# Two-layer hybrid encoder block on Trainium2: values and state products of the delta rule scan formed ahead of its steps, attention scores by pairs of heads on halves of the array

## The chip, the cores and the metric

The kernel runs on one core of one Trainium2 chip. The metric is the device time in microseconds of one execution; the median of three timed runs is given, and beside it one profiled execution.

## What is computed

Two layers over 512 tokens of width 1024. Each has a mixer of three head groups (a gated MLP, a dilated windowed attention with 6 heads, a bidirectional gated delta rule with 6 heads), an output projection, an expert layer (16 experts of 64 tokens) and a gated embedding. The change touches the delta rule and the attention. The delta rule, for one direction and per chunk of tokens (the reference uses chunks of 64, the kernel of 32):

```python
t_inv = lax.linalg.triangular_solve(lower + eye, jnp.broadcast_to(eye, lower.shape),
                                    left_side=True, lower=True, unit_diagonal=True)
u = t_inv @ (vc * bc[..., None])
w = t_inv @ (k_beta * jnp.exp(gc)[..., None])
qk = jnp.where(incl, jnp.einsum('bhntd,bhnsd->bhnts', qc, kc) * decay, 0.0)

def step(state, inp):
    q_n, k_n, u_n, w_n, g_n, qk_n = inp
    v_new = u_n - w_n @ state
    o_n = (q_n * jnp.exp(g_n)[..., None]) @ state + qk_n @ v_new
    g_last = g_n[..., -1:]
    state = state * jnp.exp(g_last)[..., None] + jnp.einsum(
        'bhtd,bhte->bhde', k_n * jnp.exp(g_last - g_n)[..., None], v_new)
    return state, o_n
```

It runs over the sequence forward and, with its own gates, backward; the two outputs are added, normalized by head and gated. The attention normalizes and rotates q and k, and its three patterns amount to one softmax over 512 keys with a fixed additive mask (`amask`), times v.

## The kernel before, in words

Tokens lie in four tiles (`t`) of 128 partitions. A projection is done in three matmuls per weight block (`mm3`): weights and activations are split in a high and a low part (`whi`, `wlo`, `xh`, `xl`), ScalarE forming the high part and GpSimd subtracting for the low one (L338, L340). Weights stream from HBM on SP's queue, each load issued when a buffer is free. Twelve buffers of 8 KB per partition ("slot") hold activations and weights in turn, two more ("gslot") the scan's operands.

The mixer of a layer goes: norm, the gated MLP, the decay terms (`gate_decay`), the delta rule's q, k, v with their short convolution (`gdn_qkv`), the products within chunks (`gdn_chunk`: pD is the decay's exponent, pG the products of k with k and of k with q), the inverse of the triangular matrices by a loop of 30 rounds on VectorE (`gdn_inv`), attention's q and k (`attn_qk`), and the transpose of the inverse (`gdn_inv_T`, tile XT).

Then two things run interleaved by `interleave`. The leading one is `gdn_scan`, 16 steps, each handling one chunk of the forward and one of the backward direction for all heads. A step: pK (L937) is k and q times the state St; tm (L940) scales it by the decay EG; rr (L944) is the values less k's part; pV (L951) multiplies by the inverse XT; vn (L955, ScalarE) copies it out; pS (L966) multiplies by the decayed k (kdec) and is added to the state, which GpSimd has decayed meanwhile (L961, L970); pO (L977) is the product within the chunk, added to q's part of tm for the output (L985, L987, L988). The filling one is a chain of attn_v (the value projection), core (the attention: scores sc L625, mask and maximum L629, exponential, scaling L634, four transposes ptp L640, and po L649 for two heads) and w_out_first (the first five blocks of the output projection, op). A fill piece returns a nominal cost, a scan piece the amount of fill owed after it (FILLS), and pieces are taken until at most 0.5 is owed; three fill pieces go first. The order so found is the order on TensorE: no piece starts ahead of the last matmul of the piece before it. After the scan come what is left of the fill, the group norm `gdn_out` (squares, `rsqrt`, two products, three transposes a tile) and `w_out_last`. The expert layer then has its own loads, which need the buffers of the mixer.

Of q, the head pair's two halves lie in two copies with the other head's 64 rows zero (L482, L483, L509, L510), so that each head's scores use all 128 rows against the shared k tile.

## Time and profile before

| | |
|---|---|
| median of 3 timed runs | 1956.84 us (1956.04 to 1957.46) |
| profiled execution | 1962.08 us, span 1960.3 us |
| mean granted TensorE clock | 0.95 |
| busy: TensorE, VectorE, ScalarE, GpSimd | 1809.5, 931.7, 523.9, 457.4 us |
| chain that ended last | TensorE 69%, VectorE 20%, ScalarE 3%, issue 3%, GpSimd 2%, DMA 2% |
| read from HBM | 461 MB |

Layer 0 takes 0 to 985 us of the span and layer 1 the rest. In layer 0 the scan and its fill run from 228 to about 400, the router to 449, where the experts' first product starts (449.7); these and the gated embedding last to 985. Busy is the time in which an engine has an instruction in work; matmuls are pipelined, so the start of one instruction to the start of the next is the price of one. A float32 matmul shows as two instructions, so 24 instructions are 12 products.

### The profile page before, as it was taken

The numbers are of one execution on the slowest core, as the hardware profiler recorded it, in microseconds if no ns is written. First come the engines' busy times: TensorE is split into PE (matmuls) and PEld (weight loads), VectorE is DVE, ScalarE is ACT, GpSimd is POOL, SyncE is SP. The second block draws the span as 40 slices with busy tenths as digits, with TensorE's granted clock in tenths as the row PEclk, the third lists the DMA queues.
The fourth block names the chain that finished last, engine by engine and source line by source line (L and its number), as shares of the span: only waits on it lengthen the run. The fifth ranks groups of instructions, "written<-read, shape, count | busy, mean of one in ns | idle before, by whom it ended". The sixth has DMA issues, their size and how long they took to land.

```text
span 1960.3 us, 30038 instructions
## 1 busy us (share of the span) xinstructions
PE 1809.5 (92%) x12216; PEld 1140.4 (58%) x12216; DVE 931.7 (48%) x2088; ACT 523.9 (27%) x1213; POOL 457.4 (23%) x402
## 2 busy tenths in 40 slices
PE   6898698979999999999989978899799999999999
PEld 5777665864344444434988767568544344443358
DVE  5879767671112121132778796776511212114126
ACT  4334444331010101102443344552311011011023
POOL 3544313320000003021645452233100000031025
PEclk9998788989999999999998977999799999999999
DMA  5212020187799999899342020202987999998991
GB/s 169 86 33 60 17 85 15 56 329 302 321 423 421 409 421 407 345 412 379 111 134 76 24 74 2 97 2 102 411 321 318 422 421 397 422 394 345 380 328 66
DMA packets 122394, 467.47 MB, mean 238 GB/s; under 512 B 11664, under 2 KB 68496, under 8 KB 75920
## 3 DMA queue, kind: packets, MB, share of 16 engines
q1 hardware_dynamic: 115168, 458.46, 59.5%
q10 hardware_dynamic: 7088, 7.09, 1.2%
q8 instruction: 96, 1.57, 0.3%
q14 instruction: 42, 0.34, 0.1%
HBM read 461.32 MB, written 4.19 MB: 237 GB/s over the span
## 4 chain that ended last, share of the span: by engine, by line
PE 69%; DVE 20%; ACT 3%; issue 3%; POOL 2%; DMA 2%; ACTq 0%; SPq 0%; DVEq 0%; POOLq 0%
PE pGt L1276 14%; PE pUp L1276 11%; PE pY L1276 10%; DVE acc L778 3%; PE xep L1206 2%; PE ysc L1295 2%; DVE rr L944 2%; PE xep L1207 2%; PE pY L1391 2%; PE pV L951 1%; PE op L348 1%; PE ysc L1296 1%; PE pgp L348 1%; PE pgp L350 1%; PE plep L1172 1%
## 5 line engine op out<-in xcount | busy, mean ns | idle before, releaser
L1276 PE MATMUL pGt<-w,xe 128*64 128x512 f32 x592 | 194.8, 607 | 0.0
L340 POOL TENSOR_TENSOR wlo<-w,whi 128x512 fp32r<-128x512 f32 (+5 forms) x66 | 162.1, 2473 | 102.9 <-ACT whi L338 71.9
L1276 PE MATMUL pUp<-w,xe 128*64 128x512 f32 x688 | 178.4, 593 | 0.0
L1343 POOL TENSOR_TENSOR x<-x,hh 128x1024 f32<-128x1024 f32 x8 | 18.8, 2356 | 620.0 <-DMA wx<-in_w_e_up_dram 310.4
L1276 PE MATMUL pY<-w,hidT 128*64 128x512 f32 x608 | 162.5, 596 | 0.2 <-ACT hidT L1350 0.2
L1360 DVE SCALAR_TENSOR_TENSOR yl<-pY,gsl,yh 128x512 fp32r<-128x512 f32 x28 | 21.0, 751 | 203.1 <-ACT yh L1359 201.5
L1301 DVE TENSOR_TENSOR x<-ysc,x 128x512 f32<-128x512 f32 x96 | 62.9, 686 | 110.5 <-PE ysc L1296 110.5
L1276 PEld LDWEIGHTS pUp<-w,xe 128*64 128x64 f32 x688 | 62.9, 137 | 89.5 <-issue 86.3
L1276 PEld LDWEIGHTS pGt<-w,xe 128*64 128x64 f32 x592 | 56.1, 137 | 99.2 <-issue 92.7
L1276 PE MATMUL pGt<-wx,xe 128*64 128x512 f32 x384 | 113.0, 599 | 0.3
L1334 DVE SCALAR_TENSOR_TENSOR hid<-sg,gsl,pUp 128x512 f32<-128x512 f32 x32 | 23.9, 748 | 169.8 <-PE pUp L1276 168.0
L1276 PEld LDWEIGHTS pY<-w,hidT 128*64 128x64 f32 x608 | 55.6, 136 | 76.2 <-issue 73.3
L1276 PE MATMUL pUp<-wx,xe 128*64 128x512 f32 x320 | 99.8, 595 | 0.0
L1276 PE MATMUL pY<-wx,hidT 128*64 128x512 f32 x288 | 86.2, 595 | 0.0
L1327 DVE SCALAR_TENSOR_TENSOR sg<-sg,pGt 128x512 f32<-128x512 f32 x32 | 21.7, 686 | 131.3 <-ACT sg L1326 131.3
L338 ACT ACTIVATE whi<-w 128x512 fp32r<-128x512 f32 (+5 forms) x66 | 68.2, 1058 | 38.5 <-PE op L349 15.8
L1326 ACT ACTIVATE sg<-pGt,gsl 128x512 f32<-128x512 f32 x32 | 21.8, 687 | 196.5 <-PE pGt L1276 194.6
L1350 ACT ACTIVATE hidT<-htp 128x512 f32<-128x512 f32 x32 | 19.0, 597 | 200.4 <-PE htp L1349 200.4
L1206 PE MATMUL xep<-OH,hh 128*128 128x256 f32 x256 | 70.1, 307 | 2.4 <-DVE OH L1194 2.4
L778 DVE SCALAR_TENSOR_TENSOR acc<-raw,pp,acc 128x512 f32<-128x512 f32 x72 | 64.3, 894 | 15.5 <-ACT acc L776 13.0
L348 PE MATMUL pgp<-whi,gTh 128*128 128x256 f32 x256 | 70.9, 281 | 0.0
L350 PE MATMUL pgp<-whi,gTl 128*128 128x256 f32 x256 | 69.8, 282 | 0.3 <-DVE gTl L279 0.3
(404 smaller groups left out, 4277.3 us busy)
## 6 DMA issues: line engine op xcount, KB each, us to landing
w<-in_w_e_up_dram SPq DMA_DIRECT2D x86, 1024.0 KB, 15.4
w<-in_w_e_down_dram SPq DMA_DIRECT2D x76, 1024.0 KB, 12.7
w<-in_w_e_gate_dram SPq DMA_DIRECT2D x74, 1024.0 KB, 15.6
wx<-in_w_e_gate_dram SPq DMA_DIRECT2D x48, 1024.0 KB, 9.9
wx<-in_w_e_up_dram SPq DMA_DIRECT2D x40, 1024.0 KB, 16.7
wx<-in_w_e_down_dram SPq DMA_DIRECT2D x36, 1024.0 KB, 12.0
wd<-in_w_e_down_dram SPq DMA_DIRECT2D x32, 512.0 KB, 8.3
w<-in_w_in_dram SPq DMA_DIRECT2D x14, 1024.0 KB, 5.2
```

Of the source, the lines that this page charges most:

```text
L338: self.nc.scalar.activation(rr_(hi[:, ks, :]), wk, AF.Copy)
L340: e.tensor_tensor(rr_(lo[:, ks, :]), wk, hi[:, ks, :], op=ALU.subtract)
L348: pe.matmul(p, lh, rh, start=first, stop=False)
L350: pe.matmul(p, ll, rh, start=False, stop=last)
L778: v.scalar_tensor_tensor(acc, raw[:, kk:kk + S], conv[:, b, kk:kk + 1], acc, op0=ALU.mult, op1=ALU.add)
L944: v.tensor_tensor(rr[kl[dr], :], vtok[kl[dr], tl, :], fl(tm[kl[dr]]), op=ALU.subtract)
L1206: pe.matmul(p, rr_(hh[:, t, ks]), OHf[:, t, :], start=(t == 0), stop=False)
L1207: pe.matmul(p, rr_(hl[:, t, ks]), OHf[:, t, :], start=False, stop=(t == NT - 1))
L1276: pe.matmul(pt[nh][64 * ei:64 * ei + 64, :], lhs[:, kk, 64 * ei:64 * ei + 64], wt[ei][k][:, nh * 512:nh * 512 + 512], start=(kk == 0), sto ...
L1295: pe.matmul(p, rr_(OT[:, t, :]), rr_(yh[:, ns]), start=True, stop=False)
L1301: v.tensor_tensor(xv, p, xv, op=ALU.add)
L1391: pe.matmul(pY[64 * ei:64 * ei + 64, :], hidT[:, 4 * half + k, 64 * ei:64 * ei + 64], wt[ei][:, k, :], start=(half + k == 0), stop=(half * ...
```

## The change

Values and state products ahead of the steps. Since vn = XT(values) - (XT k) state, both products with XT are formed per tile of 128 tokens before they are needed (`prepare`): pU is XT times the values for both directions, copied to U (the forward one over vtok, the backward one in a new slot); pW is k times XT scaled by the decay DE, copied with a minus sign into the k places of KQ, which has a copy for each direction. Two tiles are prepared ahead of the first step, the other two in pieces behind steps 0 to 3. q's decay is multiplied into KQ in `gdn_chunk` (pT, its exponential ET, a product on GpSimd). A step is then: pK, k's and q's part in separate partitions of the same tiles; vn as four sums with U on VectorE; pS and the state; pO accumulated onto q's part in pK; the output copied by ScalarE in steps 0 to 7 and added by VectorE in 8 to 15. kdec's two tiles are replaced by ktok scaled in place (forward, after pW) and kd1. `gdn_out` joins the leading chain with a yield ahead of each tile.

Attention. q is one tile with both heads; the scores of a pair are four matmuls of 64 rows by 256 columns, and the softmax of both follows. Units are pairs, with fill costs 1.1, 0.5, 0.5, 0.9 and transposes one unit behind. The value weights are split by rows into 16 pieces in three slots and one tile; the first output weights are loaded at the end of attn_v. FILLS becomes (0.5, 1.6, 0.6, 1.5).

Cut to its core:

```diff
 OWED = 0.5

 INIT = 3
-FILLS = (1.9, 1.5, 1.1)
+FILLS = (0.5, 1.6, 0.6, 1.5)
...
+        nc, parts = self.nc, []
+        for i in range(2):
+            raw, cols, nk = self.wraw.pop(0)
+            for w in raw:
+                pair = []
+                for _ in range(2):
+                    r = len(parts) * 2 + len(pair)
+                    if r == 15:
+                        tv = self.one([128, 384], "wv15")
+                    else:
+                        if r % 5 == 0:
+                            buf = self.slot("wv")
+                        tv = buf[:, 384 * (r % 5):384 * (r % 5) + 384]
+                    pair.append(tv)
+                nc.scalar.activation(rr_(pair[0]), w[:, 0], AF.Copy)
+                nc.gpsimd.tensor_tensor(rr_(pair[1]), w[:, 0], pair[0], op=ALU.subtract)
+                parts.append([rr_(a) for a in pair])
+            if i == 0:
+                self.wload(small=True)
+        return parts
...
-            wv = [self.wnext(small=True), self.wnext()]
+            self.U1 = self.slot("U1")[:, :NT * 384].rearrange("p (t n) -> p t n", t=NT)
+            wv = self.wv_rows()

             other = chain(self.attn_v(l, wv), self.core(l), self.w_out_first(l))
-            self.interleave(self.gdn_scan(l), other)
+            self.interleave(chain(self.gdn_scan(l), self.gdn_out(l)), other)
             for _ in other:
                 pass
             self.wo2 = [self.wnext() for _ in range(2)]
-            self.gdn_out(l)
         self.w_out_last(l)
...
@@ -475,12 +494,9 @@
         v, act, pe, pool_e = nc.vector, nc.scalar, nc.tensor, nc.gpsimd

         at = [self.slot("att") for _ in range(3)]
-        qT = self.qT = [a[:, 0:2 * S].rearrange("p (e n) -> p e n", e=2) for a in at]
-        kT = self.kT = [a[:, 2 * S:3 * S] for a in at]
-        self.vat = [a[:, 3 * S:].rearrange("p (t n) -> p t n", t=NT) for a in at]
-        for q in qT:
-            pool_e.memset(q[64:128, 0, :], 0.0)
-            pool_e.memset(q[0:64, 1, :], 0.0)
+        qT = self.qT = [a[:, 0:S] for a in at]
+        kT = self.kT = [a[:, S:2 * S] for a in at]
+        self.vat = [a[:, 2 * S:3 * S].rearrange("p (t n) -> p t n", t=NT) for a in at]
...
-                    act.activation(qT[b][0:64, 0, ts], pt[0:64, j], AF.Copy, scale=gT[0:64, 0:1])
-                    act.activation(qT[b][64:128, 1, ts], pt[64:128, j], AF.Copy, scale=gT[64:128, 0:1])
+                    act.activation(qT[b][:, ts], pt[:, j], AF.Copy, scale=gT[:, 0:1])
...
-        def first(j, t, hp):
-            p = self.pb([128, S], "sc")
-            pe.matmul(p, self.qT[j][:, hp, t * 128:(t + 1) * 128], self.kT[j], start=True, stop=True)
-            P = self.p1([128, S], "P")
-            mx = self.small([128, 1], "mx", 3)
-            sm_ = self.small([128, 1], "smx", 3)
+        def first(j, t):
+
+            ps = [self.pb([128, S], "sc") for _ in range(2)]
+            for half in range(2):
+                cs = slice(half * S // 2, (half + 1) * S // 2)
+                for hp, p in enumerate(ps):
+                    hl = slice(64 * hp, 64 * hp + 64)
+                    pe.matmul(p[:, cs], self.qT[j][hl, t * 128:(t + 1) * 128], self.kT[j][hl, cs], start=True, stop=True)
+            return [softmax(p, t) for p in ps]
+
+        def softmax(p, t):
+            P = mp.tile([128, S], F32, tag="p1", name="P", bufs=P1)
+            mx = self.small([128, 1], "mx", 4)
+            sm_ = self.small([128, 1], "smx", 4)
...
-        units = [(j, t, hp) for j in range(3) for t in range(NT) for hp in range(2)]
+        units = [(j, t) for j in range(3) for t in range(NT)]
         Ps = {}
-        for i in range(len(units) + 3):
+        for i in range(len(units) + 2):
             self.mark("core")
             if i < len(units):
                 Ps[i] = first(*units[i])
-                yield 0.9
-            if 0 <= i - 2 < len(units):
+                yield 1.1
+            if 0 <= i - 1 < len(units):
+                for hp in range(2):
+                    self.mark("core")
+                    second(*units[i - 1], hp, Ps[i - 1][hp])
+                    yield 0.5
+            if 0 <= i - 2:
                 self.mark("core")
-                second(*units[i - 2], Ps.pop(i - 2))
-                yield 0.5
-            if i - 3 >= 0 and units[i - 3][2]:
-                self.mark("core")
-                third(*units[i - 3][:2])
+                third(*units[i - 2])
                 yield 0.9
...
+            for dr in range(2):
+                pe.matmul(pDD[:, i, dr], self.cst(masks[dr]), g[:, :, 6 * dr:6 * dr + 6], start=True, stop=True)
+        ex = self.small([128, 192], "ex")
         act.activation(ex, pe_all, AF.Exp)
-        self.EG = ex[:, 0:96].rearrange("p (n j e) -> p n j e", j=3, e=2)
-        self.DC = ex[:, 96:192].rearrange("p (n d j) -> p n d j", d=2, j=3)
-        self.DD = ex[:, 192:240].rearrange("p (d t h) -> p d t h", d=2, t=NT)
+        self.DC = ex[:, 0:96].rearrange("p (n d j) -> p n d j", d=2, j=3)
+        self.DD, self.DE = (ex[:, 96 + 48 * i:144 + 48 * i].rearrange("p (d t h) -> p d t h", d=2, t=NT)
+                            for i in range(2))
...
-        self.kdec = [self.one([128, NT, 6, 64], f"kdec{dr}") for dr in range(2)]
+
+        self.kd1 = self.one([128, NT, 384], "kd1")
         for t in range(NT):
-            kt = ktok[:, t, :].rearrange("p (h d) -> p h d", h=6)
-            for dr in range(2):
-                pool_e.tensor_tensor(self.kdec[dr][:, t], kt, self.DD[:, dr, t, :, None].to_broadcast([128, 6, 64]),
-                                     op=ALU.mult)
+            heads = lambda a: a[:, t, :].rearrange("p (h d) -> p h d", h=6)
+            pool_e.tensor_tensor(heads(self.kd1), heads(ktok), self.DD[:, 1, t, :, None].to_broadcast([128, 6, 64]),
+                                 op=ALU.mult)
...
+            for m in range(2):
+                pT = self.pg([128, 2, 2, 3, 32], "pT")
+                for e in range(2):
+                    for par in range(2):
+                        pe.matmul(pT[64 * par:64 * par + 64, e], cim[:, 2 * m + e, :], GC[:, :, par::2, :],
+                                  start=True, stop=True)
+                ET = self.t(4, [128, 2, 2, 3, 32], "ET")
+                act.activation(ET, pT, AF.Exp)
+                qs = [a[:, :, 4 * t + 2 * m:4 * t + 2 * m + 2, :].rearrange("p j e s -> p j (e s)")
+                      .rearrange("p j (b s) -> p j b s", s=32)[:, :, 1:3, :] for a in (self.KQ[:, 0], self.KQ[:, 1])]
+                for dr in (1, 0):
+                    pool_e.tensor_tensor(qs[dr], qs[0], ET[:, :, dr].rearrange("p e j s -> p j e s"), op=ALU.mult)
```

The scan:

```diff
+        XT, QKm, vtok, ktok, DC = self.XT, self.QKm, self.vtok, self.ktok, self.DC
+        KQ, kd = self.KQ, [ktok, self.kd1]
+        o1 = self.gslot("o1")[:, :NT * 384].rearrange("p (t n) -> p t n", t=NT)
+        U = [vtok, self.U1]
...
+        def prepare(tl):
+
+            self.mark("scan")
+            ps = [self.pg([128, 6, 64], "pU") for _ in range(2)]
+            xws = []
+            for dr, p in enumerate(ps):
+                x = XT[:, dr, 6 * tl:6 * tl + 6, :]
+                xw = self.p2([128, 6, 32], "xw")
+                pool_e.tensor_tensor(xw, x, self.DE[:, dr, tl, :, None].to_broadcast([128, 6, 32]), op=ALU.mult)
+                xws.append(xw)
+                for h in range(6):
+                    for r in rows:
+                        pe.matmul(p[r, h, :], x[r, h, :], vtok[r, tl, h * 64:(h + 1) * 64], start=True, stop=True)
+            for dr, p in enumerate(ps):
+                act.activation(heads(U[dr][:, tl, :]), p, AF.Copy)
+            yield
+            self.mark("scan")
+
+            ps = [self.pg([128, 2, 3, 32], "pW") for _ in rows]
+            for j in range(3):
+                for par in range(2):
+                    h = 2 * j + par
+                    for dr, xw in enumerate(xws):
+                        for c, r in enumerate(rows):
+                            pe.matmul(ps[c][lanes[par], dr, j, :], ktok[r, tl, h * 64:(h + 1) * 64], xw[r, h, :],
+                                      start=True, stop=True)
+            for c, p in enumerate(ps):
+                ko = 32 * (c % 2)
+                act.activation(KQ[:, :, :, 4 * tl + c, ko:ko + 32], p, AF.Copy, scale=-1.0)
+            pool_e.tensor_tensor(heads(ktok[:, tl, :]), heads(ktok[:, tl, :]),
+                                 self.DD[:, 0, tl, :, None].to_broadcast([128, 6, 64]), op=ALU.mult)
+            yield
+
+        for tl in (0, NT - 1):
+            for _ in prepare(tl):
+                yield FILLS[0]
...
+        ahead = chain(*(prepare(tl) for tl in range(1, NT - 1)))
+        St = None
         for n in range(NCH):
             self.mark("scan")
+            if n == NCH // 2:
+                self.o_sum = self.gslot("o_sum")[:, :NT * 384].rearrange("p (t n) -> p t n", t=NT)
             c = n % 4
             cur = ((0, n, c, n // 4), (1, NCH - 1 - n, 3 - c, NT - 1 - n // 4))
...
+            pK = [self.pg([128, 3, 64], f"pK{par}") for par in range(2)]
+            vn = u
             if n:
-                pK = [self.pg([128, 3, 64], f"pK{par}") for par in range(2)]
...
+
+                for out, o in ((kl, 0), (ql, 1)):
+                    for j in range(3):
+                        for par, dr in quad:
+                            _, ch, cc, _ = cur[dr]
+                            ko = 32 * (cc % 2 ^ o)
+                            pe.matmul(pK[par][out[dr], j, :], KQ[lanes[par], dr, j, ch, ko:ko + 32],
+                                      St[lanes[par], dr, j, :], start=(j == 0), stop=(j == 2 and not o))
+                new = self.t(3, [128, 6, 64], "vn")
+                vn = [new, new]
+                for dr in range(2):
+                    for par in range(2):
+                        v.tensor_tensor(new[kl[dr], par::2, :], pK[par][kl[dr]], u[dr][kl[dr], par::2, :], op=ALU.add)
+                yield FILLS[1]
...
-            pV = self.pg([128, 6, 64], "pV")
-            for h in range(6):
-                for dr, ch, cc, tl in cur:
-                    pe.matmul(pV[kl[dr], h, :], XT[kl[dr], dr, 6 * tl + h, :],
-                              rhs[dr][:, h * 64:(h + 1) * 64], start=True, stop=True)
-            vn = self.t(3, [128, 6, 64], "vn")
-            for dr in range(2):
-                act.activation(vn[kl[dr]], pV[kl[dr]], AF.Copy)
-            yield FILLS[1]
...
-                        _, ch, cc, tl = cur[dr]
-                        pe.matmul(pS[dr][64 * par:64 * par + 64, j, :], kdec[dr][kl[dr], tl, 2 * j + par, :],
-                                  vn[kl[dr], 2 * j + par, :], start=True, stop=True)
+                        tl, h = cur[dr][3], 2 * j + par
+                        pe.matmul(pS[dr][lanes[par], j, :], kd[dr][kl[dr], tl, h * 64:(h + 1) * 64],
+                                  vn[dr][kl[dr], h, :], start=True, stop=True)
                 for dr in range(2):
...
-            pO = self.pg([128, 6, 64], "pO")
-            for h in range(6):
-                for dr, ch, cc, tl in cur:
-                    pe.matmul(pO[ql[dr], h, :], QKm[kl[dr], dr, 6 * tl + h, :], vn[kl[dr], h, :],
-                              start=True, stop=True)
...
-            tmp = self.t(2, [128, 384], "tmp") if n >= NCH // 2 else None
-            for dr, ch, cc, tl in cur:
...
-                else:
-                    v.tensor_tensor(tmp[kl[dr], :], fl(pO[ql[dr]]), fl(tm[ql[dr]]), op=ALU.add)
-                    pool_e.tensor_tensor(od, tmp[kl[dr], :], od, op=ALU.add)
+            for j in range(3):
+                for par, dr in quad:
+                    tl, h = cur[dr][3], 2 * j + par
+                    pe.matmul(pK[par][ql[dr], j, :], QKm[kl[dr], dr, 6 * tl + h, :], vn[dr][kl[dr], h, :],
+                              start=(n == 0 and j == 0), stop=(j == 2))
+            for par in range(2):
+                for dr, _, _, tl in cur:
+                    o = heads(o1[:, tl, :])[ql[dr], par::2, :]
+                    if n < NCH // 2:
+                        act.activation(o, pK[par][ql[dr]], AF.Copy)
+                    else:
+                        v.tensor_tensor(heads(self.o_sum[:, tl, :])[kl[dr], par::2, :], pK[par][ql[dr]], o, op=ALU.add)
             yield FILLS[2]
-        self.tap("o_sum", o_sum)
+            if next(ahead, 0) is None:
+                yield FILLS[0]
...
         for t in range(NT):
+            yield FILLS[3]
+            self.mark("gdn_out")
             ot = o_sum[:, t, :].rearrange("p (h d) -> p h d", h=6)
```

## Rows read from the trace of the kernel before

**Rows 1.** Windows by stage: start:end, length, busy (count) per engine, PEclk, DMA share, GB/s.

```profile
142.00:228.00 86.00, 64.12 (x511) 57.31 (x511) 81.43 (x169) 40.79 (x163) 39.82 (x47) 0.84 0.16 44
228.00:407.00 179.00, 164.71 (x2130) 126.69 (x2131) 118.70 (x320) 68.04 (x154) 50.30 (x43) 0.90 0.16 54
460.00:480.00 20.00, 20.00 (x116) 10.13 (x116) 3.42 (x13) 4.36 (x8) 0.00 (x0) 1.00 0.57 213
1191.00:1371.00 180.00, 163.69 (x2149) 126.26 (x2148) 123.72 (x322) 72.80 (x174) 54.20 (x47) 0.93 0.16 53
```

**Rows 2.** Waits of TensorE in 228 to 407: total us, times, longest.

```profile
PE pV L951 <- DVE rr L944: 11.3, 15, 3.9
```

**Rows 3.** Windows of 8 us, columns as in rows 1.

```profile
272.00:280.00 8.00, 4.31 (x59) 2.50 (x56) 7.85 (x17) 3.11 (x5) 5.07 (x2) 0.96 0.00 0
280.00:288.00 8.00, 8.00 (x78) 5.74 (x75) 3.02 (x9) 2.54 (x6) 0.83 (x1) 0.50 0.01 2
```

**Rows 4.** Chain of waits: start, us, what; three steps' pV, the last projection's first op.

```profile
228.19 1.49 PE pV L951 x24
...
316.75 0.85 PE pV L951 x24
...
342.71 0.85 PE pV L951 x22
...
400.89 0.50 PE op L348
```

**Rows 5.** Timeline of TensorE 290 to 306: start, us, operation, instructions.

```profile
292.01 0.86 PE L951 MATMUL pV<-rr,XT 32*32 32x64 f32 x24
292.80 1.13 PE L625 MATMUL sc<-att 128*128 128x512 f32 x2
293.86 0.74 PE L966 MATMUL pS<-vn,kdec 32*64 32x64 f32 x24
294.53 0.86 PE L977 MATMUL pO<-vn,QKm 32*32 32x64 f32 x24
295.32 0.65 PE L640 MATMUL ptp<-cst,P 128*128 128x128 f32 x4
...
296.76 0.58 PE L937 MATMUL pK<-St,KQT 64*64 64x64 f32 x24
297.27 0.66 PE L640 MATMUL ptp<-cst,P 128*128 128x128 f32 x4
297.86 1.09 PE L649 MATMUL po<-PT,att 128*64 128x128 f32 x16
298.88 1.12 PE L625 MATMUL sc<-att 128*128 128x512 f32 x2
```

**Rows 6.** Timeline of TensorE 148 to 150.

```profile
148.15 0.77 PE L875 MATMUL pG<-KQT 64*32 64x64 f32 x48
148.84 0.59 PE L858 MATMUL pD<-GC,mcst 128*128 128x192 f32 x2
149.27 0.49 PE L860 MATMUL pD<-mcst,cst 128*128 128x192 f32 x2
149.60 0.49 PE L858 MATMUL pD<-GC,mcst 128*128 128x192 f32 x2
```

**Rows 7.** Groups by form, VectorE, 228 to 407: busy us, mean ns, idle before.

```profile
L944 DVE TENSOR_TENSOR rr<-vtok,tm 32x384 f32<-32x384 f32 x30 | 23.3, 777 | 0.9
L629 DVE CUSTOM_DVE_ANT_0 P<-sc,amask 128x512 f32<-128x512 f32 x24 | 16.4, 687 | 8.8 <-PE sc L625 8.6
L634 DVE TENSOR_SCALAR P<-P,smx 128x512 f32<-128x512 f32 x24 | 12.9, 538 | 0.4
L940 DVE TENSOR_TENSOR tm<-pK,ex 128x192 f32<-128x192 f32 x30 | 9.3, 350 | 8.4 <-PE pK L937 8.4
...
L987 DVE TENSOR_TENSOR tmp<-pO,tm 32x384 f32<-32x384 f32 x16 | 8.9, 553 | 1.9 <-PE pO L977 1.5
```

**Rows 8.** Groups by form, GpSimd, 142 to 228.

```profile
L837 POOL TENSOR_TENSOR kdec<-ktok,ex 128x384 f32<-128x384 f32 x8 | 7.1, 925 | 2.3 <-DVE ex L832 2.3
```

More of the change, by code (lines that the diff above doesn't have):

```diff
@@ L36 @@
 SLOTS = 12
+P1 = 4
 WX = 5
@@ L62, in shape_constants @@
                               np.where(b[None, :] <= loc[:, None], 0.0, -30000.0)], 1)
-    lane = np.arange(64)
-    eg = np.zeros((128, 2, 2, 2, 64))
+    parts["mle"] = same & (r[:, None] <= r[None, :])
+    parts["mge"] = same & (r[:, None] >= r[None, :])
     ci = np.zeros((128, 4, 64))
-    for half in range(2):
-        for par in range(2):
-            inc = (r // C) == (2 * half + par)
-            eg[:, half, 0, par] = inc[:, None] & (loc[:, None] <= lane[None, :] % C)
-            eg[:, half, 1, par] = inc[:, None] & (loc[:, None] >= lane[None, :] % C)
     for c in range(4):
         ci[:, c] = ((r // C) == c)[:, None]
-    parts["egm"] = eg
     parts["cim"] = ci
@@ L609, in attn_v @@
                 for k in (4 * i, 4 * i + 2):
-                    self.proj_cols(p, wv[i], t, range(k, k + 2), 4 * i)
+                    ts = slice(t * 128, (t + 1) * 128)
+                    for kk in (k, k + 1):
+                        self.mm3(p, rr_(self.xh[kk // 4][:, kk % 4, ts]), rr_(self.xl[kk // 4][:, kk % 4, ts]),
+                                 wv[kk][0], wv[kk][1], kk == 0, kk == KD - 1)
                     yield 1.0
@@ L752, in gdn_qkv @@
         v, act, pe, pool_e = nc.vector, nc.scalar, nc.tensor, nc.gpsimd
-        KQT = self.KQT = self.one([128, 3, NCH, 64], "KQT")
+        KQ = self.KQ = self.one([128, 2, 3, NCH, 64], "KQT")
+        KQT = self.KQT = KQ[:, 0]
         conv = self.ppar(l, "conv").rearrange("p (b k) -> p b k", k=5)
@@ new lines, in gdn_scan @@
+        KQ, kd = self.KQ, [ktok, self.kd1]
+        o1 = self.gslot("o1")[:, :NT * 384].rearrange("p (t n) -> p t n", t=NT)
+        U = [vtok, self.U1]
+        heads = lambda a: a.rearrange("p (h d) -> p h d", h=6)
+        lanes = [slice(64 * par, 64 * par + 64) for par in range(2)]
+        rows = [slice(32 * c, 32 * c + 32) for c in range(4)]
+        quad = ((0, 0), (1, 1), (0, 1), (1, 0))
+        def prepare(tl):
[28 more added lines that the diff above has]
+            yield
@@ L948, in gdn_scan @@
-            pV = self.pg([128, 6, 64], "pV")
-            for h in range(6):
-                for dr, ch, cc, tl in cur:
-                    pe.matmul(pV[kl[dr], h, :], XT[kl[dr], dr, 6 * tl + h, :],
-                              rhs[dr][:, h * 64:(h + 1) * 64], start=True, stop=True)
-            vn = self.t(3, [128, 6, 64], "vn")
-            for dr in range(2):
-                act.activation(vn[kl[dr]], pV[kl[dr]], AF.Copy)
-            yield FILLS[1]
-            self.mark("scan")
+            kl = [rows[cc] for _, _, cc, _ in cur]
@@ new lines, in gdn_scan @@
+            ql = [rows[cc ^ 1] for _, _, cc, _ in cur]
+            u = [heads(U[dr][:, tl, :]) for dr, _, _, tl in cur]
+            pK = [self.pg([128, 3, 64], f"pK{par}") for par in range(2)]
+            vn = u
+            if n:
+                for out, o in ((kl, 0), (ql, 1)):
[11 more added lines that the diff above has]
+                yield FILLS[1]
+                self.mark("scan")
```

59 lines of the change are left out of this document (13 added, 46 removed).

## Prediction

> **What bounds the kernel now.** I read the busy shares by stage first. The two layers do the same work: the stretch from the first step of the delta scan to the end of the mixer takes 179 us in the first layer and 180 in the second, with TensorE busy 165 and 164 of them, at a mean clock of 0.90 and 0.93 [rows 1]. The 86 us ahead of it are VectorE's: it is busy 81 of them, TensorE 64. The experts behind it run on weights in flight: between 460 and 480 TensorE is busy 20.00 of 20 and the transfers have a share of 0.57, so the loads wait for buffers there. An earlier end of the mixer therefore passes through to the end nearly whole.
>
> Inside the stretch the waits of TensorE come second: 11.3 us in 15 waits of pV for rr, the longest 3.9 [rows 2]. Third the clock, in windows of 8 us: after 3.7 us without work in 272 to 280 the granted clock is 0.50 in the next 8 us (the lower level, 1.2 GHz) [rows 3]. The stretch also begins at the lower level, behind VectorE's: its first pV takes 1.49 where a later one takes 0.85 [rows 4]. So the 172.7 us from that pV (228.2) to the first instruction of the last output projection (400.9) [rows 4] hold some 15 us of idle TensorE and about as much lost to the clock; the rest is work. The same view has three steps of the scan in 316.75 to 342.71, 8.65 us each. A step is priced from starts in TensorE's timeline: pK 0.51, pV 0.79, pS 0.67, pO 0.79, together 2.76; of the attention laid between, one head's scores take 1.06, its four transposes 0.59, the product with the values of two heads 1.02 [rows 5]. By its own units (0.9, 0.5, 0.9) the loop lays 4.5 units into a step; two heads cost 4.3 us for 3.7 units, the other fills less, and I take 1.07 us a unit: 2.76 + 4.8 = 7.6 of the 8.65. VectorE needs nearly as much: tm and St 0.35 four times, rr and the two output sums 0.55 four times, and 4.5 units of attention at some 1.55 a head [rows 7], 7.4 in all. Each step is its busier engine plus 1 us of waits.
>
> **The change, part by part.** TensorE of a step: pV goes (-0.79). pK becomes 24 products on pieces of 64 rows by 32 columns instead of 12 on 64 by 64. Per instruction pK takes 21 ns (0.51 for 24), pG, a 64 by 32 piece over four column groups, 14.4 (0.69 for 48) [rows 6], and pO, two 32 by 32 pieces at a time, 33. I take 21, the form nearest in rows and columns used together: 48 x 21 = 1.0. A step is then 2.46 (1.46 for the first, which has no pK). The scan's four preparations add 4 x (48 + 48) products, 768 instructions, on 32-row pieces that the trace doesn't have in fours: at 14.4 ns 11 us, at 33 ns 25; I take 20.5, 15.7 us. The scores of two heads become four products of half the columns on 64 rows each: from 2.12 us for both (nothing gained) to 1.06 (two halves always beside one another); pK's 24 at 21 ns, where two column groups alone could give no better than half the time of one, say that row halves do overlap, so 1.06.
>
> VectorE of a step: rr and tm go, four sums of 32 by 192 come with one operand in PSUM, as tm, at 0.35 (1.4 with the queue), St stays 0.7, the output sums are ScalarE's in the first eight steps and four more of 0.35 in the last eight. The attention's 2.2 units of fill need 2.3. So 4.4 in a first-half step, 5.8 in a second-half step. rr's two stalls (mean 777 ns [rows 7] with a longest wait of 3.9) go with rr; what is late next is vn behind pK, covered by the 1.6 units between pK and pS, and St behind pS, covered by pO and 0.6 units.
>
> The sum for one layer, from 228.2. (a) Preparation and steps 0 to 4: 15.7 + 1.46 + 4 x 2.46 + the 13 pieces of attn_v left behind the three laid ahead (13.9) + 5 for the half clock at the start, which stays = 45.9. (b) Steps 5 to 7: TensorE 2.46 + 2.2 units (2.35) = 4.8, with 0.6 of waits 5.4, three times 16.2. (c) Steps 8 to 15: VectorE's 5.8 is now the larger, with 0.4 of waits 6.2, eight times 49.6. (d) The group norm is now inside the interleaving with 1.5 units ahead of each of its tiles. Its chain from the last pO (four sums 1.2, squares and reduces 1.5, some 15 small operations and two products of 0.55 as the other 384-column operations [rows 7], semaphores) is an estimate of 7 us; the fill laid ahead of its first transposes is 2.1 units, so TensorE stands for about 5, where the kernel before ran the first output projection beside the whole chain. With its transposes (4 x 0.33) and 4.5 units more: 13.1. (e) What is left of the fill: attention 36 - 30.6 = 5.4 units and the projection's 25.7, 33.3 us, + 5 because an idle time of 5 us is longer than the 3.7 that half clock followed: 38.3. Sum 163.1 against 172.7: 9.6 us less.
>
> Ahead of 228: kdec falls from eight products to four on GpSimd (4 x 0.9 less [rows 8]), six fills of zeros go, 16 products of 192 columns come, and TensorE gets 32 products of 192 columns by half the array (0.17 to 0.33 each by pD's pairs of instructions [rows 6], 5 to 10 us), ScalarE eight exponentials. All of it lies beside VectorE's 81 of 86 us, whose own operations stay, and TensorE has 22 us without work there. I take 0; ends -3 (GpSimd's queue was late at 142) and +6 (pD and pG of later tiles stand behind the new products, so VectorE waits). The value weights' split is the same eight copies and eight subtractions in other buffers; the first output weights are loaded some 16 units later, ahead of nothing on SP's queue but the loads of x, with 30 units still to run: 0, and some 5 us if their slot is late. The zero fills of q and half of its copies are off the path.
>
> Both layers: 2 x 9.6 = 19.2. The profiled execution took 1962.1 (span 1960.3), so 1942.9; the median of the three timed runs is 5.2 below that execution, hence **1937.7 us**.
>
> A rule speaks against the change. In the trace the instruction pair behind pG, which goes from 64 by 32 pieces to the full array, starts its successor after 0.43 where the next pair takes 0.33 [rows 6]: 0.10 for a change of form. The Trainium skill, "TensorEngine Tiling (Array Packing)", section "Tiling Modes", under Key Properties, says that changing the tiling mode, not just the tile, drains the engine; the trace agrees, with a drain of 0.10 us. The scores leave the full array for 64-row halves and return, 24 times a layer: 2.4 us more by row and rule together, which would make the sum 1942.5; I leave it in the range, because the other forms' changes are in their prices already.
>
> **The rivals.** (1) The pieces run four at a time (14.4 ns, as pG) and the group norm's gap doesn't lower the clock. Preparation -4.6, pK in (a) -1.3 and in (b) -0.9, (e) -5: 21.4 us a layer, 1914. For it: pG shows four column groups overlapping; against it pK, pS and pO, none of which gets there.
> (2) Slower: row pieces wait for each other. At pO's 33 ns the preparation costs 25.3 (+9.6), pK 1.58 (+2.3 in (a), +1.7 in (b)), and score halves that don't overlap +0.8 a step in (b) and (e), 5 us. That is 18.6 against the 9.6 gained, 9.0 a layer, **1975**. It decides from about 27 ns an instruction, where the gain is gone. For it: pV and pO, 32-row pieces on the diagonal, are what the preparation's first half looks like; against it pK at 21 ns with two row halves.
> (3) A new wait eats it. pK's two accumulators are now held until pO is added and the outputs are copied out: 0.79 + four evacuations of 0.35, about 2.2 us behind pS, where St is ready after 0.8. With four buffers in that ring, the next pK may wait some 0.8 more than the fill covers: 12 us over 15 steps, 8 of it visible beside VectorE in (c). Left: 1.6 a layer, 1954. For it: the ring has no spare buffer; against it pS's buffers come free early and can serve the next pK.
>
> **How the numbers follow.** Chances: the forecast 0.42 (own range 1926 to 1950), rival 1 0.28, rival 2 0.15, rival 3 0.15. Range 1900 to 1968: rival 1 with VectorE's steps shorter too, to rival 2 at two thirds; about 0.08 lies below and 0.10 above. Faster by over 0.2% (3.9 us, about what a measurement of this kernel tells from no change): 0.40 + 0.28 + 0.07 = 0.75; within it 0.08; slower 0.17, nearly all of it rival 2.
>
> **What would show it.** Right: steps 8 to 15 about 6.2 us apart with VectorE the busiest engine; no wait of 3 us for a vector operation in the scan; 96 instructions of the preparation's first half in about 2 us and of its second the same; a gap near 5 us on TensorE before the group norm's transposes with half clock behind it; the experts' first product 9 to 10 us earlier in the first layer (449.7 before). Wrong: 48 instructions of pK over 1.3 us, a score pair near 2 us, pK waiting for ScalarE's output copies, or VectorE idle ahead of the scan because pG came late. A gap in the experts that grows by what the mixer gained would refute the passing through.

## The result, and the profile after

The changed kernel takes 2034.6 us (median of 4 runs, 2030.0 to 2035.7) where the kernel before took 1957.2 beside it (4 runs): 1.039 times as long, 95% interval 1.037 to 1.041. The forecast was 1937.7, faster; its sign was wrong.

Windows by stage of the changed kernel, columns as in [rows 1]: the scan and what is laid beside it in both layers, then a stretch of the experts.

```profile
231.00:431.00 200.00, 159.50 (x2895) 132.75 (x2895) 97.74 (x318) 67.67 (x172) 37.35 (x39) 0.83 0.21 73
1222.00:1432.00 210.00, 167.42 (x2913) 139.12 (x2911) 104.82 (x321) 72.27 (x193) 42.78 (x44) 0.82 0.20 72
490.00:510.00 20.00, 20.00 (x104) 9.06 (x102) 0.00 (x0) 1.90 (x4) 0.00 (x0) 1.00 0.92 350
```

From the first product of the scan (231.3) to the first of the last projection (430.0) it is 199 us, against 172 before: there the projection's first product starts at 400.07, a little ahead of the 400.89 that [rows 4] calls the first. TensorE is busy for a smaller share of it than before (159.5 of 200 us for 164.7 of 179) and at a lower clock, 0.83 for 0.90 [rows 1]; VectorE is far from busy. So it is waits and clock, not work. The experts are as dense as before, and their first product comes 31.3 us later in the first layer (481.0 for 449.7): what the mixer loses passes through. The readings below are from the first layer; the second shows the same two largest waits (St 11.9 us in all, group norm 11.0).

Waits of TensorE, first layer, 228 to 440, columns as in [rows 2]:

```profile
PE pK L1022 <- DVE St L1043: 11.3, 7, 2.9
PE ycp L1092 <- DVE o_sum L1089: 11.0, 1, 11.0
PE op L368 <- POOL wlo L336: 4.6, 3, 2.2
PE op L367 <- ACT whi L334: 3.9, 2, 2.8
PE pW L990 <- POOL xw L974: 3.3, 1, 3.3
PE pS L1039 <- DVE vn L1028: 2.5, 2, 2.3
```

rr's waits are gone and as many us stand at pK instead, for the state St. The longest single wait is that of the group norm's transposes (ycp), 11.0 us with nothing beside it. The two op lines are output weights that come late: SP stood 94.9 us for an attention product before it could issue the second block (381.38). Then it issued five of the experts' loads, and the third block, issued behind them, took 13.0 us to land. SP's wait, its timeline, and the chain that ended last:

```profile
SPq L293 <- PE po L677: 94.9, 1, 94.9
...
381.38 0.38 SPq L293 DMA_DIRECT2D w<-in_w_out_dram  x1
381.87 21.34 SPq L1338 DMA_DIRECT2D wx<-in_w_e_gate_dram  x5
404.21 0.38 SPq L293 DMA_DIRECT2D w<-in_w_out_dram  x1
...
404.21 13.02 DMA w<-in_w_out_dram
```

Two windows of 8 us at the group norm, columns as in [rows 3], with half clock behind the gap:

```profile
368.00:376.00 8.00, 0.00 (x0) 0.00 (x0) 7.39 (x32) 2.97 (x7) 0.00 (x0) 0.62 0.00 1
376.00:384.00 8.00, 6.40 (x35) 4.73 (x36) 3.95 (x10) 3.55 (x5) 2.59 (x1) 0.52 0.11 26
```

Prices on TensorE's timeline (columns as in [rows 5]):

```profile
244.84 2.10 PE L990 MATMUL pW<-xw,ktok 32*64 32x32 f32 x96
...
251.00 1.54 PE L978 MATMUL pU<-vtok,XT 32*32 32x64 f32 x96
252.47 0.77 PE L1022 MATMUL pK<-St,KQT 64*32 64x64 f32 x48
...
355.94 1.31 PE L650 MATMUL sc<-att 64*128 64x256 f32 x8
...
360.70 0.76 PE L1022 MATMUL pK<-St,KQT 64*32 64x64 f32 x48 [2.15 <-DVE St L1043]
```

From start to start, 96 instructions of pU take 1.47 us (15 ns each), 96 of pW 2.03 (21), 48 of pK 0.71 (15). The forecast took 20.5 ns for pU and pW and 21 for pK, so pW costs what was forecast and the other two less. A pair of scores takes 1.24 us to the next operation (1.06 forecast).

### The profile page after: what moved, and what is told of

The parts are those of the page before. It is cut to its first block, busy times and chain, and to the rows that moved or that the text cites. A ratio compares the mean times of both kernels' runs of the same rounds, so it can differ in the third digit from the quotient of the medians.

```text
span 2028.2 us, 33471 instructions
## 1 busy us (share of the span) xinstructions
PE 1823.8 (90%) x13904; PEld 1170.6 (58%) x13904; DVE 886.4 (44%) x2088; ACT 526.3 (26%) x1253; POOL 448.6 (22%) x406
## 4 chain that ended last, share of the span: by engine, by line
PE 71%; DVE 18%; ACT 5%; DMA 3%; issue 2%; POOL 1%; ACTq 0%; SPq 0%; DVEq 0%; POOLq 0%
PE pGt L1350 14%; PE pUp L1350 11%; PE pY L1350 10%; DVE acc L802 3%; PE xep L1280 2%; PE ysc L1369 2%; DMA w<-in_w_out_dram 2%; PE po L677 2%; PE xep L1281 2%; PE pY L1465 2%; PE pgp L367 1%; PE pgp L369 1%; PE pgp L368 1%; PE ysc L1370 1%; PE plep L1246 1%
## 5 line engine op out<-in xcount | busy, mean ns | idle before, releaser
L1282 ACT ACTIVATE xe<-xep,pp 128x256 f32<-128x256 f32 x64 | 30.2, 474 | 155.6 <-PE xep L1281 155.6
L368 PE MATMUL pgp<-wlo,gTh 128*128 128x256 f32 x256 | 70.2, 279 | 0.0
```

Of the source, the lines that this page charges most:

```text
L368: pe.matmul(p, lh, rl, start=False, stop=False)
```

## The experiments

The kernel before took 1956.9 to 1958.2 us beside each of the runs, and each ratio is to its time beside that run. "Laying" is which fill stands where beside the scan and the group norm. Two edits of laying come up again and again. "Norm behind" is

```
-            self.interleave(chain(self.gdn_scan(l), self.gdn_out(l)), other)
+            self.interleave(self.gdn_scan(l), other)
...
             self.wo2 = [self.wnext() for _ in range(2)]
+            for _ in self.gdn_out(l):
+                pass
```

and "FILLS" is the one line with the units of fill behind each piece of the scan. "Whole rows" puts q back as two zero-padded tiles and the scores into one product of 512 columns on 128 rows a head (loops around them and the tiles of q left out):

```
-                    pe.matmul(p[:, cs], self.qT[j][hl, t * 128:(t + 1) * 128], self.kT[j][hl, cs], ...)
+                pe.matmul(p, self.qT[j][:, hp, t * 128:(t + 1) * 128], self.kT[j], start=True, stop=True)
```

**1. More fill**, on the changed kernel: `FILLS = (1.0, 2.6, 1.2, 1.5)` for `(0.5, 1.6, 0.6, 1.5)`.

> The changed kernel with more of the attention laid into the scan: FILLS (1.0, 2.6, 1.2, 1.5), 72 units of fill beside the scan and the group norm instead of 44. Theory 'left behind': the changed kernel's time went into fill that is left behind the scan while TensorE waits inside it (pK for St 11.3 us, pS for vn 2.5 in the first layer, then half clock). The waits of pK for St fall below 4 us, the last attention product ends 20 us or more before 400.7, and the time falls by 2 x 20 to about 1995. Rival 'norm in the lead': TensorE's 11.0 us at the group norm's first transposes stay, with less fill left to lay around them, so no more than 2 x 8 is won: 2018. Rival 'weights': the second block of output weights still lands late, and the time stays within 10 us of 2034.6.

Measured 1999.9, 1.0205 of before [1.0183, 1.0227]. The last attention product ends at 353 instead of 401 and pK waits 1.7 us for St instead of 11.3: 'left behind' in its mechanism and nearly in its size. The norm still stands 7.0 us, and op waits 8.7 for its weights.

```profile
PE op L367 <- ACT whi L334: 8.7, 1, 8.7
PE ycp L1092 <- DVE o_sum L1089: 7.0, 1, 7.0
...
PE pK L1022 <- DVE St L1043: 1.7, 2, 0.9
...
296.40 45.70 SPq L293 DMA_DIRECT2D w<-in_w_out_dram  x2
```

SP's last line shows something else that changed: the second block of output weights goes out at 296 instead of 381, with the norm still in the lead. So the 35 us won are not parted into cover and earlier weights.

**2. Norm behind**, on the changed kernel.

> The changed kernel with the group norm put back behind the fill (only the scan leads; the group norm's four tiles follow after the attention and the first output projection, as in the kernel before). Theory 'norm in the lead': its 11.0 us of idle TensorE and some 4 us of half clock behind it go in each layer: about 2005. Theory 'left behind': the 11 us go as well, but what is late stays late, 2010 to 2015. Rival 'weights': the two buffers of the group norm's output are no longer taken before the output weights', so the second weight load is issued before 350 instead of at 381 and both layers win some 25 us: 1985. If the norm's chain is merely moved to the end of the projection, the time stays at 2030 or above.

1991.2, 1.0171 [1.0145, 1.0196]. The 11.0 us become 2.1, and the second block of weights is issued at 312: 43 us won, more than the norm's gap and its clock alone.

```profile
PE ycp L1094 <- DVE o_sum L1091: 2.1, 1, 2.1
```

**3. A buffer back**, on the changed kernel: U1 out of the 12 shared buffers.

```
-            self.U1 = self.slot("U1")[:, :NT * 384].rearrange("p (t n) -> p t n", t=NT)
+            u03 = mp.tile([128, 2, 384], F32, tag="qk", name="U1", bufs=2)
+            self.U1 = {0: u03[:, 0], 3: u03[:, 1], 1: mp.tile([128, 384], F32, tag="wsT", name="U1", bufs=1),
+                       2: self.one([128, 384], "U1")}
```

> The changed kernel with the state products U1 kept in a freed buffer of attn_qk, in the buffer of wsT and in one small tile, so that one of the 12 shared buffers comes free when the value products are done, as in the kernel before. Nothing else differs. Theory 'weights': the second load of output weights is issued near 290 instead of 381, ahead of the experts' loads, and the projection's waits for weights (13.0 + 2.9 + 4.6 + 3.5 us in the chain of waits) go: 2 x 20 less, 1995. Theory 'left behind': the attention still ends near 400, only the projection behind it gets faster by the 8 to 10 us that TensorE has no work there: 2015 to 2020. Theory 'norm in the lead': no change, within 5 us of 2034.6.

2042.8, 1.0427 [1.0408, 1.0447], slower. SP's timeline shows that the buffer went to the first block, issued 51 us earlier than in the changed kernel, and the second waited as there:

```profile
224.93 0.42 SPq L293 DMA_DIRECT2D w<-in_w_out_dram  x1
...
384.21 0.38 SPq L293 DMA_DIRECT2D w<-in_w_out_dram  x1
```

So one buffer more is no remedy; the price of the late loads by themselves isn't measured by it.

**4. The attention alone**, on the kernel before: the changed core with its pairs, half rows and four buffers each for P and PT; FILLS (1.9, 1.5, 1.1) as before.

> The kernel before with the attention's part of the change alone: scores by pairs of heads in halves of the array, four buffers for the probabilities and four for their transposes, units by pairs; scan, group norm and FILLS as before. A pair of scores took 1.30 us in the changed kernel where two heads cost 2.12 before, 12 pairs a layer. If TensorE bounds the scan's steps, 10 us a layer are won: about 1938. If VectorE's softmax and the scan's waits set the steps, TensorE only waits longer: within 5 us of 1957. If a pair held in two accumulators starves the softmax (both score buffers are taken at once), slower: 1970 or more.

1987.0, 1.0146 [1.0124, 1.0168]: slower by 30. The pairs declare 36 units where single heads declared 44.4, so the same FILLS leave 4.6 units behind the scan where the kernel before leaves 13, and the norm is nearly bare:

```profile
PE ycp L1024 <- DVE o_sum L1021: 8.5, 1, 8.5
PE po L654 <- ACT PT L647: 5.8, 4, 2.1
```

**5. Norm behind and FILLS (1.0, 2.2, 1.0)**, on the changed kernel.

> Both edits of the first two experiments at once: the group norm behind the fill, and FILLS (1.0, 2.2, 1.0): 57 units of fill beside the scan and some 18 left behind it, where the kernel before leaves 13 to cover the group norm's chain. Theory 'the laying' (what is lost is cover: too little fill inside the scan, none around the norm): the two gains add up but for the 5 us of each that they share, 1991 - 2 x 12 = about 1967. If the scan's new form is itself slower than the old one whatever is laid around it, no more than 10 us below the better of the two: 1980 to 1990. If the fill inside the scan only makes its steps longer (VectorE bound), 1991 or more.

1951.6, 0.9953 [0.9934, 0.9972]: faster than both kernels. 83 us come from two edits that change the order and no instruction. The gains of the first two, 35 and 43, add up, and 5 more; 1967 was expected.

**6. The attention alone, fill matched**: the fourth with FILLS (1.7, 1.3, 0.95).

> The attention's part alone on the kernel before, once more, with FILLS brought down by the units that the pairs declare less (36 for 44.4): (1.7, 1.3, 0.95), so that some 13 units are again left behind the scan. Theory 'cover': the 30 us that the attention alone lost came from fill that ran out before the scan (the group norm's first transposes waited 8.5 us and the last projection began at half clock); they come back, and the 10 us a layer of cheaper scores with them: 1940 to 1957. Rival 'softmax by pairs': the pair's products with the values wait for their transposes' copies (po for PT 5.8 us in four waits) and the clock falls in the steps (0.77 to 0.82 between 304 and 352): it stays above 1975 whatever FILLS says.

1994.6, 1.0165 [1.0134, 1.0197]. ycp now waits 1.9, and nothing is won: theory 'cover' fails for the attention. The mean clock is 0.80 between 228 and 440 where it was 0.89.

**7. The scan alone**: the changed kernel with single heads on whole rows as before, norm behind, FILLS (1.0, 2.6, 1.4).

> The changed kernel's scan with the attention as before (single heads, whole array, zero-padded q), the group norm behind the fill, and FILLS (1.0, 2.6, 1.4), which leave some 14 of the 83 units behind the scan. Theory 'the laying': the scan's new form is no slower than the old one by itself, 1950 to 1965. Rival 'the pairs are the loss': as the attention alone lost 30 us, this one is faster than the kernel before, 1940 or less. Rival 'the preparation is the loss': some 20 us of preparation a layer with a clock at its start that is half, and no gain in the steps: 1985 or more.

1957.9, 0.9993 [0.9976, 1.0009]: the new scan by itself, with its fill set anew, costs and wins nothing that can be measured.

**8. Buffers early**: norm behind, but yTc's two buffers taken at the scan's end again (`chain(self.gdn_scan(l), self.take())`).

> The second experiment (group norm behind the fill, FILLS as in the changed kernel) with one thing put back: the two buffers of the group norm's output are taken at the scan's end again, ahead of the output weights', although the norm runs last. It parts the norm's 11 us of idle TensorE from the order of the loads. Theory 'weights late': the second block of output weights lands at about 385 again, behind experts' loads, and most of the 43 us that the second experiment won are lost: 2015 to 2030. Theory 'norm in the lead': the idle time stays away, the loads cost what the projection waits beyond the attention, 5 us a layer at most: 1991 to 2001.

1989.7, 1.0173 [1.0136, 1.0210], as the second. The second block of weights was issued at 308.5 all the same. So this edit doesn't bring the late weights back, and the run doesn't price them either. No trace shows from when the two buffers were held; their first write is at 414.3.

**9. Single heads on half rows**: the seventh with each head's scores on its own 64 rows.

```
-            pe.matmul(p, self.qT[j][:, hp, t * 128:(t + 1) * 128], self.kT[j], start=True, stop=True)
+            hl = slice(64 * hp, 64 * hp + 64)
+            pe.matmul(p, self.qT[j][hl, t * 128:(t + 1) * 128], self.kT[j][hl], start=True, stop=True)
```

> The seventh experiment (new scan, group norm behind, single heads) with each head's scores taken on its own 64 rows of the array in one product of 512 columns instead of on all 128 with zeros in half of q; no zero fills, half of the copies of q. The order and the units are unchanged, so it parts the half rows from the pairing. If the lower clock of the runs with pairs comes from the half rows (half the array idle in the scores), the granted clock between 272 and 352 falls from 1.00 towards 0.8 and the time rises by 10 or more, to 1968. If it comes from the pairs' bursts (two accumulators, softmax of two heads at once), it stays within 5 us of the 1957.9, or a little below.

1986.7, 1.0113 [1.0039, 1.0187]; three runs took 1986 to 1991 at a mean clock of 0.94, one 1962.4 at 0.954. Windows of the seventh, then of this run:

```profile
304.00:320.00 16.00, 15.86 (x313) 10.82 (x298) 13.27 (x45) 12.58 (x30) 1.91 (x3) 1.00 0.01 4
320.00:336.00 16.00, 14.60 (x256) 9.39 (x255) 14.63 (x39) 6.60 (x16) 5.72 (x3) 1.00 0.01 3
```

```profile
304.00:320.00 16.00, 16.00 (x234) 10.07 (x230) 9.87 (x32) 9.51 (x22) 1.66 (x2) 0.75 0.01 3
320.00:336.00 16.00, 16.00 (x174) 9.37 (x173) 8.97 (x30) 5.68 (x14) 1.66 (x2) 0.57 0.01 3
```

TensorE is busy all 32 us and the clock is lower. Windows of 4 us of this run show it fall with no gap ahead (TensorE is busy all the time from 292 to 340):

```profile
316.00:320.00 4.00, 4.00 (x92) 2.74 (x84) 3.50 (x13) 1.98 (x5) 0.00 (x0) 1.00 0.00 0
320.00:324.00 4.00, 4.00 (x70) 2.16 (x72) 2.19 (x7) 2.69 (x7) 0.83 (x1) 0.76 0.02 4
324.00:328.00 4.00, 4.00 (x61) 3.16 (x44) 2.44 (x10) 1.69 (x4) 0.00 (x0) 0.50 0.01 2
```

So it is the half rows, not the pairing. Why one run of four lost hardly anything stays open.

**10. More cover**: the fifth with four pieces ahead of the scan and FILLS (1.5, 2.4, 1.0).

> The fifth experiment with more fill around the preparation: four pieces of the value products ahead of the scan instead of three, FILLS (1.5, 2.4, 1.0): 64 units beside the scan, some 9.7 left behind it for the group norm's chain. Theory 'the laying': the preparation's waits (pW for xw 2.3, pK for St 5.2) shrink, and 9.7 units are just enough for the norm: 1940 to 1950. If the cover behind the scan is what counts, the norm's first transposes wait 3 us or more and the last projection begins at half clock: 1955 to 1965.

1966.1, 1.0039 [1.0022, 1.0056]. The 9.7 units left behind the scan are too few: ycp waits 4.9 us (0.5 in the fifth), and 384 to 400 has a clock of 0.79 where the fifth had 1.00.

**11. Half rows alone**, on the kernel before: the edit of the ninth.

> The kernel before with one thing changed: each head's scores on its own 64 rows of the array, one product of 512 columns, q in one tile without zeros (no zero fills, half of the copies of q). Scan, group norm, order, units and FILLS are untouched. If products on half the rows bring the lower clock by themselves, as between 304 and 368 in the ninth experiment (0.50 to 0.75 with TensorE busy all the time), the clock between 264 and 352 falls below the 0.60 to 1.00 of before and the time rises to 1975 to 1985, most of what the attention alone lost. If the pairing was that loss, the time stays at 1952 to 1958.

1994.8, 1.0189 [1.0164, 1.0214]: 38 us lost by a change that takes instructions away (zero fills, copies of q) and adds none. TensorE's waits in the first layer (228 to 400) fall as well, from 15.4 us to 4.6, so it isn't gaps that grew. The kernel before, then this one, in the attention:

```profile
320.00:336.00 16.00, 15.05 (x248) 10.37 (x244) 13.00 (x39) 8.15 (x20) 5.78 (x6) 1.00 0.01 2
336.00:352.00 16.00, 14.75 (x238) 9.68 (x238) 13.87 (x40) 8.81 (x21) 5.71 (x6) 1.00 0.01 2
352.00:368.00 16.00, 15.21 (x261) 12.88 (x256) 9.13 (x25) 4.98 (x11) 8.66 (x7) 1.00 0.16 51
```

```profile
320.00:336.00 16.00, 16.00 (x140) 10.05 (x140) 7.50 (x23) 4.66 (x11) 2.82 (x3) 0.50 0.00 1
336.00:352.00 16.00, 16.00 (x145) 9.59 (x146) 7.63 (x22) 5.88 (x12) 2.80 (x3) 0.50 0.00 1
352.00:368.00 16.00, 16.00 (x175) 10.80 (x171) 7.97 (x24) 5.25 (x12) 3.71 (x4) 0.50 0.00 1
```

48 us on end without a gap at the lower level (1.2 GHz), and some 40% fewer instructions in them.

**12. Pairs on whole rows**: the fifth with whole rows.

> The fifth experiment (new scan, pairs of heads, group norm behind, 57 units beside the scan) with the pair's scores taken on all 128 rows again, two products of 512 columns on zero-padded q; order, units and FILLS as there. A pair costs 0.8 us more of TensorE, 10 us a layer at full clock. If half rows bring the lower clock, these 10 us come back as clock (0.50 to 0.86 between 280 and 352 there, 0.9 or more here): 1945 to 1958. If they don't, the time rises by most of 2 x 10: 1965 to 1972.

1948.9, 0.9958 [0.9943, 0.9973], not told apart from the fifth. Each pair costs more, and 336 to 352 (the fifth, then this) shows what pays for it; pK's waits for St, 5.2 us in the fifth, are gone as well:

```profile
336.00:352.00 16.00, 15.45 (x243) 11.89 (x241) 10.00 (x34) 3.04 (x8) 5.86 (x3) 0.50 0.15 43
```

```profile
336.00:352.00 16.00, 14.06 (x252) 9.09 (x250) 13.00 (x45) 5.64 (x14) 5.90 (x4) 0.95 0.14 44
```

**13. The changed kernel on whole rows**, nothing else.

> The changed kernel with one thing undone: the pair's scores on all 128 rows again (two products of 512 columns on zero-padded q). Group norm in the lead and FILLS stay. If the half rows' clock is most of what the changed kernel lost, 30 us or more come back: 2005 or less. If the laying is, TensorE pays 0.8 us a pair more where it waits anyway and the clock falls after gaps as it did: 2020 to 2040. If the two add up as in the kernel before (38 us), 1997.

2014.1, 1.0272 [1.0242, 1.0303]: 20 us come back, between the cases. Norm and late weights are as they were (ycp 11.2, second block at 374.5), but pK waits 1.5 us for St instead of 11.3:

```profile
PE pK L1023 <- DVE St L1044: 1.5, 3, 0.9
```

The longer scores cover St, so what whole rows give back here is cover as well as clock.

**14 and 15. Zero fills late**: the twelfth with q's zero fills moved into attn_v, and the same with FILLS (1.0, 2.4, 1.1).

> The twelfth experiment with q's six zero fills moved from ahead of the scan into the value products (behind the second tile), off GpSimd's queue while VectorE works on the inverse: there VectorE's 30 products T took 813 ns each in the twelfth run where they took 648 in the fifth, and the scan began 6 us later. If the zero fills are what slowed them, the scan begins near 229 instead of 235 and the time falls by 5 to 12, to 1937 to 1944. If it is GpSimd's other work of that stretch, the same time: 1945 to 1950.

> The fourteenth with FILLS (1.0, 2.4, 1.1), 62 units beside the scan instead of 57, some 13 left behind it as in the kernel before. With whole rows TensorE is the busier engine in the scan's steps, so the steps grow by what is laid in and the end is the same unless waits shrink (po for PT 6.0, pK 2.0): within 4 us of the fourteenth; if the waits shrink, 3 to 6 us less.

1948.5, 0.9952 [0.9936, 0.9967], and 1955.5, 0.9978 [0.9951, 1.0005]. In the fourteenth the last transposes ahead of the scan (XT) begin 5.8 us earlier than in the twelfth (224.9 for 230.7). But the value products laid ahead of the scan then wait 2.5 us for their weights from GpSimd, and the first pK comes only 1.9 earlier; no gain over the twelfth.

## Why the prediction was wrong, step by step

Together, the runs make a table of four (us):

| | norm in the lead, 44 units | norm behind, 57 units |
|---|---|---|
| half rows | 2034.6 | 1951.6 |
| whole rows | 2014.1 | 1948.9 |

The laying, with the earlier output weights that come with it, is worth 83 or 65 us. The half rows cost 20 in the bad laying and 3 in the good one, where 3 is not told from nothing. Two things failed: the sum treated gaps as small constants beside work, and it priced the score halves by their columns at full clock. None of the three rivals held either.

The terms for the first layer, forecast and measured, from the first product to the start of pK in steps 5 and 8, the last outputs, the last ycp and the last projection:

| | forecast | measured | |
|---|---|---|---|
| start of the stage | 0 (-3 to +6) | 3.1 | VectorE waits 7.7 us for ScalarE's E, 2.0 before |
| (a) to step 5 | 45.9 | 55.3 | |
| (b) steps 5 to 7 | 16.2 | 23.1 | 7.7 a step for 5.4 |
| (c) steps 8 to 15 | 49.6 | 55.1 | 6.9 a step for 6.2 |
| (d) group norm | 13.1 | 27.6 | |
| (e) the rest | 38.3 | 37.7 | |

- **(b) and (c), wrong.** "St behind pS, covered by pO and 0.6 units" is the sentence that failed: that cover is 0.8 + 0.6 us, and pK waited for St in seven steps, 11.3 us together. In these steps the chain pK, vn, pS, St sets the pace and not an engine; VectorE, forecast as (c)'s bound, is busy 13.0 us or less of each 16 between 304 and 368. More fill between, or longer scores, removes the wait (1.7 us in run 1, 1.5 in run 13). The sign "no wait of 3 us" missed it, as the longest is 2.9.
- **(d), wrong in size.** A gap of 5 was forecast and 11.0 came, with attention laid between the tiles at half clock. The expected sign was there: the group norm with no cover. Behind the fill it costs 2.1 (run 2).
- **(e), right by luck.** Its 5 us of half clock didn't come where they were put: the half clock fell in (d), and from 384 to 416 the clock is 1.00. In their place TensorE waited 5.0 us for output weights, with 0.61 in the window around that wait (416 to 424).
- **Loads "0, and some 5 us if their slot is late", wrong.** The slot was late: the second block was issued at 381, before at 259. In runs 2, 5 and 8, with the norm behind, it wasn't, and neither in run 1, with the norm in the lead and more fill (296). Which use of a buffer makes the difference stays open: freeing U1's (run 3) and taking yTc's early (run 8) changed nothing, and the cost of late loads alone wasn't measured.
- **Scores 1.06 a pair, near in time and wrong in worth.** 1.24 was measured at full clock and 2.06 at half clock, and the sum has no term for that clock: half rows cost 38 us on the kernel before, at 0.50 for 48 us where it had 1.00 (run 11). The 0.18 above the forecast has room for the two changes of form at 0.10 each that the forecast read in [rows 6]. The Trainium skill, "TensorEngine Tiling (Array Packing)", section "Tiling Modes", says that a change of tiling mode drains the engine; no run here shows a drain apart.
- **The preparation and pK, right.** At full clock 3.5 us for each of four preparations against 3.9; rival 2 (pieces wait for each other) is refuted, and rival 1's price per piece was nearer for pU and pK. Rival 3 doesn't occur: pK waits for St, not for buffers.
- **(a), wrong by its covers.** The half clock at the start was in the sum (the first pU takes 2.78 us, a later one 1.54). Not in it are 7.0 us in which TensorE stands: 3.3 at pW for xw on GpSimd, 2.1 ahead of a value product for nothing that the profile shows, 1.6 in smaller waits. The other 2.4 of the 9.4 us above the forecast stay open.
- **Passing through to the end, right.** The experts start 31.3 us later in the first layer, and the first store of its output comes 30.6 later (1010.9 for 980.3).

With good laying the change is worth 0.5% (1951.6 us against 1958.1 beside it), about a third of the 19 us forecast. No run gave the kernel before another laying, so how much of that is the change's own isn't shown.

## What to carry to other kernels

A change that shortens a scan's steps also changes what must be laid into them: count the longest chain of a step and the bare stretches (a norm, the first weights) in microseconds of cover, and set the fill to that before judging the change. Leave enough fill behind the lead for the chain that follows it: 13 to 18 units were enough here, 9.7 and 4.6 were not. Before products are cut to half the array, look at the granted clock of a stretch of them.

## What the runs showed of the hardware

Scores on 64 of the 128 rows brought TensorE's granted clock to 0.50 for 48 us on end with the engine busy all the time; the same scores on 128 rows, half of them zeros, ran at 1.00 in the same place (run 11, on the kernel before). It came again on the new scan (run 9, where three runs of four were slower), and pairs on half rows lose about as much on the kernel before (run 6). What about the half rows brings it, fewer rows or more changes of form, isn't parted. By the Trainium skill, "TensorE: Matmul & The Clock Gate", section "What's actually happening", the lower level is the default and that of an engine that has been idle. These rows differ, as TensorE shows no idle time in them, and the measurement decides.

Four 32 by 32 pieces on the diagonal overlap: pU's take 15 ns an instruction, where pO's, two at a time, take 33 [rows 5]. pW's, 32 rows by 64 columns, take 21.
